# An encoder layer's first modulation vectors computed by column quarters, with the activations loaded from a second DMA queue

## Chip, core and metric

One core of a Trainium2 chip runs the kernel. The metric is the device time of one execution in microseconds, given as the median of three runs. TensorE (PE in the rows, PEld for its weight loads), VectorE (DVE), ScalarE (ACT), GpSimd (POOL) and SyncE (SP) run beside each other and meet at semaphores; transfers are issued from the queues of SP or ACT and carried out by 16 DMA engines. TensorE runs at one of two clocks, 1.2 or 2.4 GHz, and the rows give the granted one as a share of the higher.

## What is computed

One layer of a bidirectional encoder over 1280 tokens (1024 of a sample, 256 of a prompt), width 1024, in float32. Only its beginning matters here:

```python
mod = jax.nn.silu(c) @ ada_w + ada_b
shift1, scale1, gate1, shift2, scale2, gate2 = jnp.split(mod[:, None, :], N_MOD, axis=-1)
h = rms_norm(x, norm_mix_g) * (1 + scale1) + shift1
proj = h @ w_in
```

`ada_w` is 1024 x 6144. The first two vectors, `shift1` and `scale1`, take its first 2048 columns (8 MB), and everything after them needs `h`. Convolution, attention, the output projection and a feed-forward block follow; they are the same in both kernels.

## The kernel before

Tokens are cut into ten tiles of 128 (`xt`, tile t), grouped into chunks c = 0 (tiles 0 to 3), c = 1 (4 to 7) and c = 2 (8 and 9); the width is cut into eight slices of 128, k = 0 to 7. A program order written out by hand decides what stands in each engine's queue; each engine takes its instructions in that order, and a waiting one holds up all behind it.

- **Modulation.** `ada_load(k)` (line 130) loads 128 rows of `ada_w` by 2048 columns, 1 MB, in rows of 8 KB. `ada_products` (line 220) multiplies them by the activated condition `c32`: four matmuls of 512 columns, each into its own 32 partitions of one PSUM bank `aps`. All eight k must be in before `mod_finish` (line 203) can copy the bank out (`rows`), turn it by four transposes (`mps`) and add the bias. `scale_gain` (line 235) then makes the scale vectors `A1`.
- **Normalising x.** `x_load` (line 247) loads a tile of 0.5 MB, `x_norm` (line 252) squares and sums it on ACT and forms the inverse root on POOL, and `x_scale` (line 261) multiplies it on DVE.
- **Turning x.** `h_turn(c, k)` (line 318) transposes slice k of the chunk's tiles on PE; `modulate` (line 264) reads the PSUM bank on ACT with scale and bias (`hf`), makes the high half `Hh` on DVE and the low half `Hl` on DVE for even k and on POOL for odd k.
- **First products.** `passes` (line 327) multiplies one slice by the split weights in three matmuls: wh by Hh, wh by Hl, wl by Hh. Lines 376 to 384 do this for chunks 0 and 1 and the first two column blocks of `w_in` (`w_first`), six matmuls to each (c, k), with three transposed slices ahead of the products. Chunk 2's products (`fmb`) come after.
- **Weights of `w_in`.** They are streamed by `Stream` (line 32): a column block of 128 is loaded as `wr` (0.5 MB, in rows of 512 bytes), copied to `wh` on ACT, and the rest `wl` is formed on POOL.

All these loads are issued from SP's queue, in program order. A transfer takes one of eight completion semaphores, and it is not issued until the transfer that used that semaphore before has landed; these waits stand in the issuing queue like any other.

Of the kernel before, what the change touches and what calls it, by code (L numbers as in the profile page):

```python
# [70 lines left out]
def encoder_kernel(tc, x_prompt, x_sample, c_prompt, c_sample, ada_w, ada_b, norm_mix_g, w_in,  # L71
# [55 lines left out]
    wada = ada_w[0].rearrange("(k p) n -> k p n", p=128)  # L127
    ada_raw = {}

    def ada_load(k):  # L130
        raw = sp.tile([128, 2048], F32, tag="ar", name="ar", bufs=4)
        nc.sync.dma_start(raw, wada[k][:, 0:2048])
        ada_raw[k] = raw

    ada_load(0)
    ident = co.tile([128, 128], F32, name="ident")
# [5 lines left out]
    for k in range(1, 4):  # L142
        ada_load(k)
# [96 lines left out]
    h_cm, hp = pool("h1", side="right")  # L240
    Hh = [hp.tile([128, KD, n], F32R, name=f"Hh{c}") for c, (_, n) in enumerate(CH)]
    Hl = [hp.tile([128, KD, n], F32R, name=f"Hl{c}") for c, (_, n) in enumerate(CH)]
    xp_cm, xp = pool("xp", side="right")
    xts = {}
    xrs = {}

    def x_load(t):
        xt = xp.tile([128, D], F32, tag="xt", name="xt", bufs=8)
        nc.sync.dma_start(xt, x_rows(t))
        xts[t] = xt  # L250

# [30 lines left out]
    aps = bank("t", "aps", 4)  # L282
    for k in range(8):
        raw = ada_raw.pop(k)
        for n in range(4):
            ada_products(aps, k, n, raw[:, n * 512:(n + 1) * 512])
        if k + 4 < 8:
            ada_load(k + 4)
        if k == 3:
            for r0, n, src in vsrc:  # L290
                nc.sync.dma_start(vrow[r0:r0 + n], src)
            for t in range(4):
                x_load(t)
# [3 lines left out]
    A1 = co.tile([128, 8, 2], F32, name="A1")

    x_norm(0)
    turn = mod_finish(0, aps, xp)  # L300
    x_norm(1)
    x_scale(0)
    turn()
    scale_gain(1, "nm", A1)
    x_norm(2)
    x_scale(1)
    x_norm(3)
    x_scale(2)
    x_load(4)
    x_load(5)  # L310
    x_load(6)
    x_load(7)
# [29 lines left out]
    def fmajor(w, Xh, Xl, nk, between=None):  # L342
# [12 lines left out]
    turns = [(c, k) for c in range(3) for k in range(KD)]
    nxt = [0]

    def turns_to(n):
        while nxt[0] < min(n, len(turns)):
# [3 lines left out]
            if c == 0 and k < 4:  # L363
                x_norm(4 + k)
                if k > 0:
                    x_scale(3 + k)
# [1364 lines left out]
```

## Time and profile before

| | |
|---|---|
| median of three runs | 1901.2 us (1901.16 to 1902.71) |
| the profiled execution's own time | 1901.46 us |
| its span | 1899.5 us |
| mean granted clock of TensorE | 0.991 |
| PE busy | 1844.8 us, 97% of the span |
| DVE, ACT, POOL busy | 1073.2, 682.4, 657.2 us |

The span runs from the first to the last instruction of the profiled execution; 1.96 us of its time lie outside. A busy PE may still run at the lower clock, and matmuls are pipelined, so the pace of matmuls is read from the distance between their starts and not from the length of one record.

### The profile page before, as it was taken

To read this page: it belongs to the slowest core of one execution; us is meant where nothing else is said; L and a number is where in the kernel's file an instruction comes from. 1 tells how busy PE (TensorE), PEld (TensorE's weight loads), DVE (VectorE), ACT (ScalarE), POOL (GpSimd) and SP (SyncE) were. 2 spreads that over 40 slices of the span, in tenths; PEclk is the share of its full clock that TensorE was granted. 3 is DMA by queue.
4 is the path that set the end of the run, shared out by engine and by line. 5 is a ranking of instruction groups with operands and counts; after the bars stand their busy time and mean duration, and the time that the engine had idled before them with its cause. 6 is when DMAs were issued, how large, how long until landed. Compare 5 with 4: busy or idle time off the path is not lost.

```text
span 1899.5 us, 24511 instructions
## 1 busy us (share of the span) xinstructions
PE 1844.8 (97%) x9468; PEld 1539.1 (81%) x9468; DVE 1073.2 (57%) x1396; ACT 682.4 (36%) x1132; POOL 657.2 (35%) x491
## 2 busy tenths in 40 slices
PE   5999999999999999998999989999999999999998
PEld 2888777888997888877788878888888888888886
DVE  2799996524346777776455753333334555555557
ACT  3411111221346877774233444444444111111112
POOL 3321121421321343437322013333445444344343
PEclk7999999999999999999999999999999999999999
DMA  8313452227131211116632223222226332233224
GB/s 312 112 43 108 171 185 99 70 99 250 51 98 61 56 41 39 46 56 222 204 122 78 84 100 97 93 95 95 88 91 214 117 100 76 75 100 100 75 93 154
DMA packets 120933, 207.54 MB, mean 109 GB/s; under 512 B 10946, under 2 KB 78355, under 8 KB 119794
## 3 DMA queue, kind: packets, MB, share of 16 engines
q1 hardware_dynamic: 103106, 167.32, 27.7%
q10 hardware_dynamic: 17712, 38.67, 5.2%
q8 instruction: 74, 1.21, 0.3%
q14 instruction: 41, 0.34, 0.1%
HBM read 151.83 MB, written 54.12 MB: 108 GB/s over the span
## 4 chain that ended last, share of the span: by engine, by line
PE 85%; DVE 4%; DMA 4%; ACT 3%; POOL 2%; issue 1%; SPq 1%; ACTq 0%; POOLq 0%; DVEq 0%
PE dn_ps L1583 23%; PE up_ps L1444 14%; PE fma L328 5%; PE fma L330 5%; PE fma L329 5%; PE wo_ps L1198 5%; PE tp L866 3%; PE up_ps L330 2%; PE up_ps L329 2%; PE up_ps L328 2%; PE fmb L328 1%; PE fmb L330 1%; PE fmb L329 1%; PE pq L668 1%; PE pq L666 1%
## 5 line engine op out<-in xcount | busy, mean ns | idle before, releaser
L160 POOL TENSOR_TENSOR wl<-wr,wh 128x1024 fp32r<-128x1024 f32 (+1 forms) x100 | 235.4, 2354 | 728.7 <-ACT wh L156 705.8
L1598 DVE TENSOR_TENSOR acc<-acc,dn_ps 128x512 f32<-128x512 f32 x260 | 178.7, 687 | 174.9 <-PE dn_ps L1583 174.9
L1583 PE MATMUL dn_ps<-wh,gl 128*128 128x512 f32 x640 | 249.1, 389 | 0.9 <-POOL gl L160 0.9
L1583 PE MATMUL dn_ps<-wh,gh 128*128 128x512 f32 x640 | 249.0, 389 | 0.0
L1583 PE MATMUL dn_ps<-wl,gh 128*128 128x512 f32 x640 | 249.0, 389 | 0.0
L156 ACT ACTIVATE wh<-wr 128x1024 fp32r<-128x1024 f32 (+1 forms) x104 | 102.9, 991 | 381.5 <-PE dn_ps L1583 291.0
L412 DVE SCALAR_TENSOR_TENSOR z<-u,dwt,z 128x1310 f32<-128x1310 f32 x120 | 220.8, 1840 | 4.3
L328 PE MATMUL fma<-Hh,wh 128*128 128x512 f32 x384 | 154.9, 403 | 0.3 <-DVE Hh L158 0.3
L329 PE MATMUL fma<-Hl,wh 128*128 128x512 f32 x384 | 150.6, 392 | 2.0 <-DVE Hl L160 2.0
L330 PE MATMUL fma<-Hh,wl 128*128 128x512 f32 x384 | 150.5, 392 | 0.0
L1583 PEld LDWEIGHTS dn_ps<-wh,gl 128*128 128x128 f32 x640 | 120.1, 188 | 26.5 <-POOL gl L160 1.4
L1583 PEld LDWEIGHTS dn_ps<-wl,gh 128*128 128x128 f32 x640 | 120.1, 188 | 24.9
L1583 PEld LDWEIGHTS dn_ps<-wh,gh 128*128 128x128 f32 x640 | 120.1, 188 | 24.8
L160 DVE TENSOR_TENSOR Pl<-tp,Ph 128x512 fp32r<-128x512 f32 x144 | 92.8, 649 | 20.2 <-ACT Ph L156 19.1
L160 POOL TENSOR_TENSOR gl<-gr,gh 128x1280 fp32r<-128x1280 f32 x32 | 94.7, 2960 | 11.9 <-DMA up_d<-r 9.7
L328 PE MATMUL up_ps<-Mh,wh 128*128 128x256 f32 (+1 forms) x320 | 97.4, 304 | 0.8 <-ACT hf L266 0.8
L329 PE MATMUL up_ps<-Ml,wh 128*128 128x256 f32 (+1 forms) x320 | 97.4, 304 | 0.0
L330 PE MATMUL up_ps<-Mh,wl 128*128 128x256 f32 (+1 forms) x320 | 97.4, 304 | 0.0
L156 ACT ACTIVATE Ph<-tp 128x512 fp32r<-128x512 f32 x144 | 82.4, 574 | 36.0 <-PE tp L866 33.2
L1444 PE MATMUL up_ps<-Mh,wh 128*128 128x512 f32 x224 | 88.2, 394 | 5.4 <-ACT p L1457 5.4
L328 PEld LDWEIGHTS fma<-Hh,wh 128*128 128x128 f32 x384 | 72.6, 189 | 23.3 <-issue 5.0
L1444 PE MATMUL up_ps<-Ml,wh 128*128 128x512 f32 x224 | 88.0, 393 | 0.0
(327 smaller groups left out, 4306.6 us busy)
## 6 DMA issues: line engine op xcount, KB each, us to landing
gr<-up_d SPq DMA_DIRECT2D x32, 640.0 KB
adr<-in_ada_w_dram SPq DMA_DIRECT2D x32, 512.0 KB
wr<-in_w_mlp_up_dram SPq DMA_DIRECT2D x32, 512.0 KB
up_d<-r ACTq DMA_DIRECT2D x64, 256.0 KB
wr<-in_w_mlp_down_dram SPq DMA_DIRECT2D x32, 512.0 KB
wr<-in_w_in_dram SPq DMA_DIRECT2D x24, 512.0 KB
ar<-in_ada_w_dram SPq DMA_DIRECT2D x8, 1024.0 KB
sig_a<-sgg ACTq DMA_DIRECT2D x8, 640.0 KB
```

What stands on the lines that cost most here:

```text
L156: nc.scalar.activation(h, raw, AF.Copy)
L160: e.tensor_tensor(l, raw, h.bitcast(F32), op=ALU.subtract)
L328: nc.tensor.matmul(o, lhsT=wh, rhs=xh, start=first, stop=False)
L329: nc.tensor.matmul(o, lhsT=wh, rhs=xl, start=False, stop=False)
L330: nc.tensor.matmul(o, lhsT=wl, rhs=xh, start=False, stop=last)
L412: nc.vector.scalar_tensor_tensor(out=z[j], in0=u[j][:, t:t + ZW], scalar=dwt[:, j, t:t + 1], in1=z[j], op0=ALU.mult, op1=ALU.add)
L666: nc.tensor.matmul(pq, lhsT=xh, rhs=wh, start=(k == 0), stop=False)
L866: nc.tensor.transpose(tp[:, i * 128:(i + 1) * 128], st_[n]["P"][i][:, k * 128:(k + 1) * 128], ident)
L1198: nc.tensor.matmul(pp[hf], lhsT=a, rhs=wo[k][b][:, hf * 512:hf * 512 + 512], start=(k == 0 and s == 0), stop=(k == KD - 1 and s == 2))
L1444: nc.tensor.matmul(out, lhsT=l_, rhs=r_[:, k, :], start=(a and s == 0), stop=(b and s == 2), skip_group_check=more)
L1583: nc.tensor.matmul(pds[hf], lhsT=l_, rhs=r_, start=(i == 0 and s == 0), stop=(i == nf - 1 and s == 2), skip_group_check=bool(early))
L1598: nc.vector.tensor_add(acc[t][:, cs], acc[t][:, cs], pds[hf])
```

## The change

The first 2048 columns of `ada_w` are loaded by quarters of each vector's columns: quarter q is two tiles of [128, 8, 256], all 1024 rows by 256 columns of `shift1` and of `scale1`, 1 MB each, in rows of 1 KB. `ada_quarter(q)` multiplies all eight k of a quarter (32 matmuls of 128 columns), copies the bank, transposes it once, and gives the slices k = 2q and 2q + 1 of `mods[0]`, `mods[1]` and `A1`. The transposed slices and the first products of these two k follow before the next quarter. x is loaded from ACT's queue, with ten buffers in place of eight; the first four tiles are loaded at the start, the others on the way. The third and fourth weight block are loaded after the last quarter of `ada_w`.

```diff
+    wcol = ada_w[0].rearrange("(k p) n -> p k n", p=128)
-    def ada_load(k):
-        raw = sp.tile([128, 2048], F32, tag="ar", name="ar", bufs=4)
-        nc.sync.dma_start(raw, wada[k][:, 0:2048])
-        ada_raw[k] = raw
+    def ada_load(q):
+        if q < 4:
+            ada_raw[q] = []
+            for m in range(2):
+                raw = sp.tile([128, KD, 256], F32, tag="ar", name="ar", bufs=4)
+                nc.sync.dma_start(raw, wcol[:, :, m * D + q * 256:m * D + q * 256 + 256])
+                ada_raw[q].append(raw)
     ada_load(0)
...
+        xt = xp.tile([128, D], F32, tag="xt", name="xt", bufs=10)
+        nc.scalar.dma_start(xt, x_rows(t))
...
+    for t in range(4):
+        x_load(t)
...
-    aps = bank("t", "aps", 4)
-    for k in range(8):
-        raw = ada_raw.pop(k)
-        for n in range(4):
-            ada_products(aps, k, n, raw[:, n * 512:(n + 1) * 512])
...
+    for r0, n, src in vsrc:
+        nc.sync.dma_start(vrow[r0:r0 + n], src)
+    WS.prefetch()
+    WS.raw_bufs = 0
+    ada_load(1)
+    for t in range(4, 8):
+        x_load(t)
...
+    def x_ready(t):
+        x_norm(t)
+        x_scale(t)
+
+    def ada_quarter(q):
+        raw = ada_raw.pop(q)
+        aps = bank("t", "aps", 4, (128, 128))
+        for k in range(KD):
+            for n in range(4):
+                nc.tensor.matmul(aps[n * 32:n * 32 + 32, :], lhsT=c32[:, k, :],
+                                 rhs=raw[n // 2][:, k, (n % 2) * 128:(n % 2) * 128 + 128],
+                                 start=(k == 0), stop=(k == KD - 1))
+        if q == 0:
             v_turn()
+        ada_load(q + 2)
+        rows = xp.tile([128, 128], F32, tag="rows", name="rows", bufs=2)
+        nc.scalar.activation(rows, aps, AF.Copy)
+        mps = bank("t", "mps", 4, (128, 128))
+        nc.tensor.transpose(mps, rows, ident)
...
+    for t in range(4):
+        x_ready(t)
+    w_first = [WS.get(R_in[0]), WS.get(R_in[1], 0)]
     dwrow = sp.tile([CK, CW], F32, name="dwrow")
-    nc.sync.dma_start(dwrow, conv_dw[0])
-    x_scale(3)
-    w_first = [WS.get(R_in[0]), WS.get(R_in[1], 0)]
+    nc.scalar.dma_start(dwrow, conv_dw[0])
+    x_load(8)
+    x_load(9)
...
+    for q in range(4):
+        k0, k1 = 2 * q, 2 * q + 1
+        ada_quarter(q)
+        h_turn(0, k0)
+        h_turn(0, k1)
+        if q == 0:
+            for t in range(4, 8):
+                x_ready(t)
+        if q == 1:
+            x_ready(8)
+            x_ready(9)
+        h_turn(1, k0)
+        first_two(0, k0)
+        h_turn(1, k1)
+        first_two(0, k1)
+        if q > 1:
+            h_turn(2, 4 * q - 8)
+            h_turn(2, 4 * q - 7)
+        first_two(1, k0)
+        if q > 1:
+            h_turn(2, 4 * q - 6)
+        first_two(1, k1)
+        if q > 1:
+            h_turn(2, 4 * q - 5)
+    WS.raw_bufs = 2
+    WS.prefetch()
```

`first_two(c, k)` is the six matmuls of lines 380 to 383. On ACT, from the first squares on, the kernel before has this order (`junk,ss<-xt` is the square of an x tile, `rows` the copy of the modulation bank, `wh` a weight's high half, `hf` the modulated slice):

```order
L256 ACTIVATE junk,ss<-xt 128x1024
L206 ACTIVATE rows<-aps 128x512
L256 ACTIVATE junk,ss<-xt 128x1024 x3
L156 ACTIVATE wh<-wr 128x1024 x2
L266 ACTIVATE hf<-xt_ps,mod_118,A_200 128x512
L256 ACTIVATE junk,ss<-xt 128x1024
L266 ACTIVATE hf<-xt_ps,mod_118,A_200 128x512
L256 ACTIVATE junk,ss<-xt 128x1024
L266 ACTIVATE hf<-xt_ps,mod_118,A_200 128x512
```

The changed kernel has this in the same place of ACT's queue, from the loads of tiles 4 to 7 on:

```order
L150 DMA xt<-in_x_sample_dram 128x1024 x4
L261 ACTIVATE junk,ss<-xt 128x1024 x4
L173 ACTIVATE wh<-wr 128x1024 x2
L330 DMA dwrow<-in_conv_dw_dram 31x512
L150 DMA xt<-in_x_prompt_dram 128x1024 x2
L312 ACTIVATE rows<-aps 128x128
L271 ACTIVATE hf<-xt_ps,mod_134,A_164 128x512 x2
L261 ACTIVATE junk,ss<-xt 128x1024 x4
L271 ACTIVATE hf<-xt_ps,mod_134,A_164 128x512 x2
L312 ACTIVATE rows<-aps 128x128
```

The squares of tiles 0 to 3, both weight halves and three DMA issues now stand ahead of the first `rows`, and the squares of tiles 4 to 7 stand in one piece between the second and the third `hf`.

The next piece is SP's queue in the changed kernel from the first quarter to the second; in brackets are the semaphores waited for. `ar` is a half of a quarter of `ada_w`, `vrow` the small vectors, `wr` the weights; DMAHW3 and DMAHW6 are first used by the two halves of the first quarter, DMAHW0, 4, 5 and 7 by x tiles 0 to 3:

```order
L137 DMA ar_91<-in_ada_w_dram 128x8x256
L137 DMA ar_93<-in_ada_w_dram 128x8x256
L288 DMA vrow_124<-in_norm_mix_g_dram 8x128 [waits DMAHW0_49]
...
L288 DMA vrow_124<-in_conv_dw_b_dram 4x128 [waits DMAHW3_49]
L288 DMA vrow_124<-in_conv_ln_g_dram 4x128 [waits DMAHW4_49]
L288 DMA vrow_124<-in_conv_ln_b_dram 4x128 [waits DMAHW5_49]
...
L288 DMA vrow_124<-in_ada_b_dram 48x128 [waits DMAHW1_49]
L184 DMA wr_148<-in_w_in_dram 128x8x128 [waits DMAHW3_49]
L184 DMA wr_150<-in_w_in_dram 128x8x128 [waits DMAHW5_49]
L137 DMA ar_152<-in_ada_w_dram 128x8x256 [waits DMAHW6_49]
L137 DMA ar_154<-in_ada_w_dram 128x8x256 [waits DMAHW7_49]
```

And ACT's queue in the changed kernel at the loads of tiles 4 to 7 (`xt_156` to `xt_162`), ahead of the first square:

```order
L150 DMA xt_156<-in_x_sample_dram 128x1024
L150 DMA xt_158<-in_x_sample_dram 128x1024 [waits DMAHW6_49]
L150 DMA xt_160<-in_x_sample_dram 128x1024 [waits DMAHW2_49]
L150 DMA xt_162<-in_x_sample_dram 128x1024 [waits DMAHW4_49]
L261 ACTIVATE junk_165,ss_166<-xt_107 128x1024 [waits DMAHW0_49]
```

The load of tile 5 (`xt_158`) waits for the second half of the first quarter to land, that of tile 7 (`xt_162`) for a `vrow` that SP issues after the first half has landed; the first square stands behind them.

On PE, from the modulation products on, the kernel before has this order (`xt_ps` are transposes of x; Hh_127 and Hl_130 are chunk 0's halves):

```order
L222 MATMUL aps<-ar,c_100 32x512 x32
...
L211 MATMUL mps<-ident,rows 128x128 x4
L323 MATMUL xt_ps<-ident,xt 128x128 x12
L328 MATMUL fma<-Hh_127,wh 128x512
L329 MATMUL fma<-Hl_130,wh 128x512
L330 MATMUL fma<-Hh_127,wl 128x512
...
L323 MATMUL xt_ps<-ident,xt 128x128 x8
```

The changed kernel has this on PE where the first quarter's products end and the second quarter begins (Hh_98 and Hl_101 are chunk 0's halves, Hh_99 chunk 1's):

```order
L346 MATMUL fma<-Hh_99,wl 128x512
L305 MATMUL aps<-ar,c_122 32x128 x32
L314 MATMUL mps<-ident,rows 128x128
L339 MATMUL xt_ps<-ident,xt 128x128 x12
L344 MATMUL fma<-Hh_98,wh 128x512
L345 MATMUL fma<-Hl_101,wh 128x512
L346 MATMUL fma<-Hh_98,wl 128x512
...
L339 MATMUL xt_ps<-ident,xt 128x128 x4
```

Between two quarters' products PE now has 32 modulation matmuls, one transpose of `rows`, and twelve transposes of x, and the first product after them needs an `hf` made from that `rows`.

## Rows read from the trace of the kernel before

**Rows 1.** From the page, the head of the profile page: span and instructions, then TensorE's (PE) busy time, share of the span and instructions.

```profile
span 1899.5 us, 24511 instructions
...
PE 1844.8 (97%) x9468; PEld 1539.1 (81%) x9468; DVE 1073.2 (57%) x1396; ACT 682.4 (36%) x1132; POOL 657.2 (35%) x491
```

**Rows 2.** From the trace, busy time by stretch (start:end, its length; then busy us and count on PE, PEld, DVE, ACT and POOL; the granted TensorE clock as a share of full; the share of the DMA engines; GB/s).

```profile
6.46:25.70 19.24, 14.53 (x65) 1.71 (x65) 0.03 (x1) 0.00 (x0) 0.00 (x0) 0.82 0.90 373
25.70:37.94 12.24, 4.73 (x16) 3.05 (x16) 4.49 (x10) 8.67 (x14) 6.16 (x10) 0.62 1.05 385
37.94:45.72 7.78, 5.81 (x17) 4.55 (x18) 7.19 (x8) 5.20 (x10) 7.23 (x9) 0.50 0.64 197
45.72:73.53 27.81, 27.07 (x149) 22.14 (x148) 20.18 (x34) 16.16 (x27) 13.95 (x16) 1.00 0.17 58
...
76.70:200.00 123.30, 123.14 (x657) 102.79 (x657) 118.84 (x74) 17.62 (x21) 29.79 (x22) 1.00 0.30 95
```

**Rows 3.** From the trace, the chain that ended last, from 23 to 46 us: start, length, and the work (queue, engine or transfer) that it went through.

```profile
15.47 8.00 DMA ar<-in_ada_w_dram
...
26.23 9.04 DMA wr<-in_w_in_dram
...
35.29 1.06 ACT wh L156
...
37.92 2.74 DVE Hl L160
...
40.70 0.80 PE fma L329
41.50 0.43 PE fma L330
...
43.21 1.71 PE xt_ps L323 x8
```

**Rows 4.** From the trace, the DMA engines from 0 to 40 us in slices of one microsecond: the rate of each slice in GB/s.

```profile
GB/s 0 4 135 229 418 451 410 426 434 434 410 426 434 434 410 426 442 434 401 442 434 426 349 4 49 225 393 389 352 381 372 329 346 378 422 406 426 422 323 284
```

**Rows 5.** From the trace, PE from 73 to 78 us: the last product of the two large chunks and the first of the small one.

```profile
73.52 0.39 PE L330 MATMUL fma<-Hh,wl 128*128 128x512 f32 x1
73.75 0.28 PE L328 MATMUL fmb<-Hh,wh 128*128 128x256 f32 x1
```

**Rows 6.** From the trace, transfers issued from SyncE's queue (SPq), in order of time: start, length of the issuing, destination and source, count.

```profile
23.85 1.84 SPq L249 DMA_DIRECT2D xt<-in_x_sample_dram  x4
25.74 2.54 SPq L167 DMA_DIRECT2D wr<-in_w_in_dram  x2
28.32 5.42 SPq L249 DMA_DIRECT2D xt<-in_x_sample_dram  x4
```

**Rows 7.** From the trace, all engines from 28 to 36 us, in order of time: start, length, engine, line, operation, operands, count, and in brackets what the engine had waited for.

```profile
28.50 0.58 ACT L206 ACTIVATE rows<-aps 128x512 f32<-128x512 f32 x1
...
30.28 0.25 DVE L217 TENSOR_TENSOR mod<-mps,vt 128x16 f32<-128x16 f32 x2
...
30.57 0.17 DVE L237 SCALAR_TENSOR_TENSOR A<-mod,vt 128x16 f32<-128x16 f32 x1
...
31.07 1.06 ACT L256 ACTIVATE junk<-xt 128x1024 f32<-128x1024 f32 x1 [0.96 <-DMA xt<-in_x_sample_dram]
...
32.36 1.06 ACT L256 ACTIVATE junk<-xt 128x1024 f32<-128x1024 f32 x1
...
33.32 0.19 ACT L256 ACTIVATION_READ_ACCUMULATOR junk<-xt 128x1 f32 x1
...
34.04 0.55 POOL L181 TENSOR_TENSOR rs<-rs,neghalf 128x1 f32<-128x1 f32 x1
34.62 0.75 DVE L262 TENSOR_SCALAR xt<-xt,rs 128x1024 f32<-128x1024 f32 x1 [0.71 <-POOL rs L181]
```

**Rows 8.** From the trace, the matmuls that transpose x, over the first 76 us: count, then shortest, median and longest in ns, and the first and last start.

```profile
L323 PE MATMUL xt_ps<-ident,xt x80: 270/273/477, 30.4 to 70.9; 128*128 128x128 f32 x80
```

**Rows 9.** From the trace, all engines from 43 to 51 us: the modulation step (hf) and its split into a high and a low half.

```profile
43.12 0.41 DVE L158 CAST Hh<-hf 128x512 fp32r<-128x512 f32 x1
...
43.57 0.69 DVE L160 TENSOR_TENSOR Hl<-hf,Hh 128x512 fp32r<-128x512 f32 x1
...
44.16 0.78 ACT L266 ACTIVATE hf<-xt_ps,mod,A 128x512 f32<-128x512 f32 x1 [1.60 <-PE xt_ps L323]
...
45.48 1.29 POOL L160 TENSOR_TENSOR Hl<-hf,Hh 128x512 fp32r<-128x512 f32 x1
```

**Rows 10.** From the trace, the chain from 45.7 to 50 us: product matmuls and the transposes of x at full clock.

```profile
47.18 0.23 PE fma L328
47.41 0.23 PE fma L329
...
48.57 0.87 PE xt_ps L323 x8
```

**Rows 11.** From the trace, PE from 18.5 to 21 us: the modulation products of one eighth of the rows (four matmuls of 512 columns, two records each), with the clock at half.

```profile
18.60 1.94 PE L222 MATMUL aps<-ar,c 128*32 128x512 f32 x8 [1.37 <-DMA ar<-in_ada_w_dram]
```

**Rows 12.** From the trace, PE from 162.9 to 164.5 us: the same four matmuls of a later modulation row, at full clock.

```profile
163.15 1.06 PE L222 MATMUL adps<-adr,c 128*32 128x512 f32 x8
164.15 0.50 PE L328 MATMUL fma<-Hh,wh 128*128 128x512 f32 x1
```

More of the change, by code (lines that the diff above doesn't have):

```diff
@@ L141, in encoder_kernel @@
     nc.gpsimd.memset(c32, 0.0)
-    for k in range(1, 4):
-        ada_load(k)
     vrow = sp.tile([81, 128], F32, name="vrow")
@@ L237, in scale_gain @@
         nc.vector.scalar_tensor_tensor(out=out, in0=mods[m], scalar=1.0, in1=g, op0=ALU.add, op1=ALU.mult)
[L240 to L250, printed above, removed]
     def x_norm(t):
@@ L297, in encoder_kernel @@
[L297 to L312, printed above, removed]
+    for r0, n, src in vsrc:
[5 more added lines that the diff above has]
+        x_load(t)
+    A1 = co.tile([128, 8, 2], F32, name="A1")
@@ new lines, in x_ready @@
+    def x_ready(t):
[10 more added lines that the diff above has]
+        if q == 0:
+            v_turn()
+        ada_load(q + 2)
[3 more added lines that the diff above has]
+        nc.tensor.transpose(mps, rows, ident)
+        ks = slice(2 * q, 2 * q + 2)
+        pv = mps.rearrange("p (m b x) -> p m b x", m=2, b=2)
+        for m in range(2):
+            b0 = VO["ab"] + m * 8 + 2 * q
+            nc.vector.tensor_tensor(mods[m][:, ks, :], pv[:, m, :, 0:2],
+                                    vt[:, b0:b0 + 2].unsqueeze(2).to_broadcast([128, 2, 2]), op=ALU.add)
+        g0 = VO["nm"] + 2 * q
+        nc.vector.scalar_tensor_tensor(out=A1[:, ks, :], in0=mods[1][:, ks, :], scalar=1.0,
+                                       in1=vt[:, g0:g0 + 2].unsqueeze(2).to_broadcast([128, 2, 2]),
+                                       op0=ALU.add, op1=ALU.mult)
@@ L352, in fmajor, with first_two @@
         return pa, pb
[L355 to L359, printed above, removed]
-            c, k = turns[nxt[0]]
-            nxt[0] += 1
-            h_turn(c, k)
[L363 to L366, printed above, removed]
-            if c == 0 and k == 4:
-                x_scale(7)
-            if c == 0 and k == 7:
-                x_load(8)
-                x_load(9)
-            if c == 1 and k in (0, 1):
-                x_norm(8 + k)
-                x_scale(8 + k)
     pas = [bank("a", "fma", 2, (128, 1024)) for _ in range(2)]
     pb0 = bank("t", "fmb", 4, (128, 256))
-    turns_to(3)
-    for c in range(2):
-        for k in range(KD):
-            for i in range(2):
-                wh, wl = w_first[i]
-                passes(pas[i][:, c * 512:(c + 1) * 512], wh[:, k, :], wl[:, k, :], Hh[c][:, k, :], Hl[c][:, k, :],
-                       k == 0, k == KD - 1)
-            turns_to(3 + (3 * (c * KD + k + 1) + 1) // 2)
-    turns_to(24)
+    def first_two(c, k):
+        for i in range(2):
+            wh, wl = w_first[i]
+            passes(pas[i][:, c * 512:(c + 1) * 512], wh[:, k, :], wl[:, k, :], Hh[c][:, k, :], Hl[c][:, k, :],
+                   k == 0, k == KD - 1)
+    for q in range(4):
[24 more added lines that the diff above has]
+    WS.prefetch()
     for k in range(KD):
```

17 lines of the change are left out of this document (8 added, 9 removed).

## The prediction

> **What bounds the kernel now.** I read the page's head first: PE is busy for 97% of a span of 1899.5 us [rows 1], so only work on PE's path counts. Then the stretches at the start, where the change lies. Until 37.94 us PE does the modulation products and waits [rows 2]; the first product of `passes` stands at 37.94. From there to 45.72 the clock is at half; from 45.72 to 73.53 PE is busy for 27.07 of 27.81 us at full clock, and after 76.70 for 123.14 of 123.30 [rows 2]. So once the products run, PE is the bound, and nothing later has slack in which a shift of this beginning could vanish: what the first stage gains or loses the kernel gains or loses. The chain says what holds the first product: the load of the eight 1 MB pieces up to 23.47 us, x and the first weights behind it up to 35.27, the weight split, the first `hf`, and then a `Hl` of 2.74 us [rows 3]. The transfers come at 426 to 434 GB/s with rows of 8 KB, at 352 to 393 with x's rows of 4 KB (slices 26 to 29), and at 329 to 346 with the weights' 512 bytes (slices 31 and 32) [rows 4]. The stage's end, by which I measure, is the first `fmb`, at 73.75 us [rows 5].
>
> **When the first product comes after the change.** The PE order puts the transposes of tiles 4 to 7 ahead of it, and ACT's queue puts nearly everything ahead of those, so I add up ACT's queue.
>
> The first quarter (2.10 MB) and tiles 0 to 4 (2.62 MB) are in flight together, 4.72 MB. Rows of 1 KB are not in the trace; bounds are 430 GB/s and 335 [rows 4], and I take 385, between x's rate and the weights'. From about 2.9 us on, where the rate rises, that is 12.3 us: the quarter's second half lands at **15.2 us** (13.9 to 17.0). ACT cannot issue tile 5 before that, and its squares stand behind these issues.
>
> The Trainium skill, "DMA: Bandwidth & Descriptors", Specifications, states that transfers run at line rate from 512 bytes a row on. By that the landing would be at 13.9 and the sum below 1.3 us less; the slices with 512-byte rows, at 329 to 346, do not agree with it. The same page (Issuing engines are not separate DMA queues) says that a second queue saves only issue time, since all transfers share 16 engines; the trace agrees in so far as one queue already fills them, with a share of 1.05 [rows 2].
>
> From 15.2 on, on ACT: three issues at 0.46 (SP takes 1.84 for four [rows 6]), 16.6. Four squares at a pitch of 1.29 (31.07 to 32.36 [rows 7]), 21.8. The two `wh` of 1.06 [rows 3]; their loads are issued only when small vectors queued behind the first quarter have landed, so at about 16.6, and share the engines with tiles 5 to 7: 2.62 MB at 370 GB/s from 17 on are in at 24.1, so the second `wh` ends at 25.2 (23.9 if nothing is waited for). Three issues, 26.6. `rows`, 128 of 512 columns of a 0.58 us copy, about 0.3; one transpose at half clock 0.48 [rows 8]; modulation and scale vectors 0.46 (30.28 to 30.74 [rows 7]): 27.8. Two `hf` of 0.78 [rows 9], 29.4. The four squares of tiles 4 to 7, 5.2: 34.6. Then the last tile's root and scaling, from the read-out's end at 33.51 to 35.37 in the trace [rows 7], 1.9, and its transpose at half clock, 0.2. The first product starts at **36.7 us** (34.1 to 38.5), 1.2 us earlier than before. The loads have become much earlier, but most of that is lost, because ACT's list of about 21.5 us starts only once the first quarter is in.
>
> **What PE then has to do.**
> - Products and transposes that were there before: 96 matmuls at a pitch of 0.231 and 68 transposes at 0.109 [rows 10], 22.2 + 7.4 = **29.6 us**. Before the change the same work took 73.75 - 37.94 = 35.8 us, 6.2 of them lost to the half clock and the long `Hl`.
> - Half clock at the beginning. The chain has a product at 0.43 there [rows 3]. In the kernel before, products ran without a break from 40.70, and the clock rose at 45.72 [rows 2, 3]: 5.0 us at half pace, **2.5 us** lost. I take the same.
> - The modulation products of quarters 1 to 3, which used to run under the loads. At full clock four matmuls of 512 columns take 1.06 us, at half 1.94 [rows 11, 12]; a quarter is eight such groups at a fourth of the columns, 2.1 or 3.9. Shorter matmuls may hide their weight loads less well; I take 2.5, nearer to the full-clock row. Three times, **7.5 us** (6.4 to 11.6). The first quarter's products lie under ACT's list and cost nothing.
> - A gap behind each of these. The next product needs `rows` (0.3), a transpose (0.27 [rows 8]), modulation and scale (0.46), `hf` (0.78), `Hh` (0.41) and some six handovers of 0.03 (34.59 to 34.62 [rows 7]): 2.4 us after the last modulation product. Twelve transposes, 1.3, fill part of it. Its second matmul then waits for `Hl` on DVE, 0.69 against 0.23 [rows 9, 10]. 1.1 + 0.5 = 1.6 us, three times **5.0 us** with the handovers. If other work filled it, nothing; at half clock about 2.5 each.
> - Quarter 1 alone has the squares of tiles 8 and 9 on ACT (2.6) ahead of chunk 1's `hf`, and their scaling on DVE, behind POOL's `Hl` of 1.29 [rows 9], ahead of chunk 1's `Hh`. Chunk 1's products come 1.5 us late, and its two low halves cost some 0.9 more: **2.4 us** (0 to 4).
>
> The loads bound none of this: the second quarter is in by about 31 us and the third by about 39, and PE asks for them at about 45 and 58; the fourth is issued when the second's products are done, at about 47, and is in by 55, against some 71. The weight blocks 2 and 3 follow it and are split only after the stage. `v_turn` lies under ACT's list as well.
>
> **Sum.** 29.6 + 2.5 + 7.5 + 5.0 + 2.4 = 47.0 us. The first `fmb` comes at 36.7 + 47.0 = 83.7 us in place of 73.75: 9.9 us later. With 1901.46 for the profiled execution that is 1911.4; the median of the runs lies 0.26 below it: **1911 us**, slower by 0.5%. My measure of no change is 0.2%, 3.8 us.
>
> **Rivals.**
> - *The clock falls in the gaps.* After PE had stood still the trace has the clock at 0.62 of full from 25.70 to 37.94 and at half to 45.72 [rows 2]. Against it: from 45.72 on short waits of PE left the clock at full [rows 2]. If each of the three gaps brings a stretch like the first, 2.5 us each, the time is 1918.5. Chance 0.14.
> - *The gaps close and the start is early.* The landing at 13.9, weights that are not waited for (first product at 34.1), modulation products at 2.1 each, and half of the 7.4 us of gaps and waits gone: 34.1 + 29.6 + 2.5 + 6.4 + 3.7 = 76.3, 2.6 us later than before, 1904, no change that can be measured. For it: DVE and POOL have room; against it: each step of the gap needs the one before. Chance 0.16.
> - *Faster: ACT's list starts while the first quarter is still coming.* Tiles 0 to 3 land from about 6 us on, and were ACT not held by the issue of tiles 5 to 7, its squares would be done 5 to 7 us sooner. With 47.0 us of work behind it, the first product has to come before 26.7 us for the kernel to gain, and before 22.9 for 0.2%. From the list's 21.5 us that means a start at 5.2 and 1.4 us, by when 4.72 MB cannot be in at any rate of [rows 4]; so the work behind would have to be shorter as well, close to the 29.6 + 2.5 + 6.4 = 38.5 us that remain without any gap. With a first product 6 us earlier, 30.7, and 38.5 behind it the stage ends at 69.2, 4.5 us earlier: 1896.7. Chance 0.07.
> - *The second queue does not do what it says.* Only tiles 0 to 4 run beside the first quarter; tiles 5 to 7 wait for it through the semaphores. That is in the sum already.
>
> **How the numbers follow.** The forecast (slower, 1906 to 1916) has 0.63, the fallen clock 0.14, both slower: 0.77. Within 0.2% has 0.16, faster 0.07. The predicted time is the forecast's. The range leaves out the faster case, the lower half of the unchanged one and a part of the fallen clock: 1903.5 to 1918.5.
>
> **What the profile would show.** The square of tile 0 at about 16.6 us and not at 6; the first `fma` product at 34 to 38.5; 32 modulation matmuls in 2 to 4 us ahead of each later quarter; behind each a PE gap ended by `Hh` or `Hl`; the first `fmb` near 84 us; all after it as before, moved by one amount. I am wrong if the first product stands below 30 us, if the clock is at half after some 42 us, if PE waits for an `ar` load in quarters 1 to 3, or if the later stages are not moved by what the first lost.

## The result, and the profile after

| | before | after |
|---|---|---|
| median | 1901.23 us (4 runs) | 1915.49 us (4 runs, 1913.59 to 1916.98) |
| ratio, 95% interval | | 1.0071 [1.0056, 1.0085] |
| span of the profiled execution | 1899.5 us | 1911.5 us |
| first product | 37.94 us | 38.66 us |
| first `fmb` | 73.75 us | 85.71 us |

The change makes the kernel slower by 0.7%. A second series of five gave 1913.7 us (below); the median of the nine is **1914.1**, and the experiments are compared with that.

The head of the page after, span and PE's busy time:

```profile
span 1911.5 us, 24904 instructions
...
PE 1843.7 (96%) x9660; PEld 1546.2 (81%) x9660; DVE 1067.5 (56%) x1405; ACT 682.9 (36%) x1135; POOL 658.2 (34%) x491
```

PE is busy for 1.1 us less than before ([rows 1] has 1844.8 us) and the span is 12.0 us longer: the time went into standing still. Where, the first 90 us show.

ACT after, in order of time (start, length, operation, operands, count; in brackets the idle time and what ended it):

```profile
14.96 1.30 ACTq L150 DMA_DIRECT2D xt<-in_x_sample_dram  x3
16.30 1.06 ACT L261 ACTIVATE junk<-xt 128x1024 f32<-128x1024 f32 x1 [10.29 <-DMA vrow<-in_kv_norm_g_dram]
...
22.84 1.06 ACT L173 ACTIVATE wh<-wr 128x1024 fp32r<-128x1024 f32 x1 [1.84 <-DMA wr<-in_w_in_dram]
24.41 1.06 ACT L173 ACTIVATE wh<-wr 128x1024 fp32r<-128x1024 f32 x1 [0.51 <-DMA wr<-in_w_in_dram]
...
25.82 0.28 ACT L312 ACTIVATE rows<-aps 128x128 f32<-128x128 f32 x1 [0.36 <-issue]
...
33.61 1.06 ACT L261 ACTIVATE junk<-xt 128x1024 f32<-128x1024 f32 x1
```

The first square stands at 16.30 us, behind three transfers that ACT issues from 14.96 to 16.26 (ACTq); the second `wh` ends at 25.47, `rows` stands at 25.82, the last square of tiles 4 to 7 begins at 33.61. What follows it, all engines from 34.5 us on:

```profile
34.57 0.18 ACT L261 ACTIVATION_READ_ACCUMULATOR junk<-xt 128x1 f32 x1
34.80 0.75 DVE L267 TENSOR_SCALAR xt<-xt,rs 128x1024 f32<-128x1024 f32 x1 [0.72 <-POOL rs L198]
34.85 0.75 POOL L197 TENSOR_SCALAR rs<-ss 128x1 f32<-128x1 f32 x1
...
35.68 0.55 POOL L198 TENSOR_TENSOR rs<-rs,neghalf 128x1 f32<-128x1 f32 x1
36.26 0.75 DVE L267 TENSOR_SCALAR xt<-xt,rs 128x1024 f32<-128x1024 f32 x1 [0.71 <-POOL rs L198]
...
37.73 0.75 DVE L267 TENSOR_SCALAR xt<-xt,rs 128x1024 f32<-128x1024 f32 x1 [0.71 <-DMA ar<-in_ada_w_dram]
...
38.54 0.47 PE L339 MATMUL xt_ps<-ident,xt 128*128 128x128 f32 x1 [0.99 <-DVE xt L267]
...
38.66 0.77 PE L344 MATMUL fma<-Hh,wh 128*128 128x512 f32 x1
```

The square's sum is read out until 34.75. Each scaling on DVE (`xt`) waits for its root on POOL (`rs`); the last row names a load, but the root before it ended at 37.70, 0.03 us earlier. POOL's 128x1 TENSOR_SCALAR takes 0.75 us where a scaling runs beside it, and 0.19 where none does (32.47, below). So the tiles come every 1.47 us, the last one 3.9 us after the last square, and the first product with it, at 38.66. Before, it stood at 37.94 [rows 3].

PE after (aps: modulation products; 64 records are one quarter's 32 matmuls):

```profile
14.98 3.63 PE L305 MATMUL aps<-ar,c 128*32 128x128 f32 x60 [1.97 <-DMA ar<-in_ada_w_dram]
...
47.31 1.95 PE L305 MATMUL aps<-ar,c 128*32 128x128 f32 x64
49.69 0.33 PE L314 MATMUL mps<-ident,rows 128*128 128x128 f32 x1 [0.42 <-ACT rows L312]
...
51.89 0.51 PE L344 MATMUL fma<-Hh,wh 128*128 128x512 f32 x1 [0.56 <-DVE Hh L175]
52.62 0.50 PE L345 MATMUL fma<-Hl,wh 128*128 128x512 f32 x1 [0.22 <-DVE Hl L177]
...
57.83 0.50 PE L344 MATMUL fma<-Hh,wh 128*128 128x512 f32 x1 [1.96 <-DVE Hh L175]
...
61.62 1.96 PE L305 MATMUL aps<-ar,c 128*32 128x128 f32 x64
...
73.75 1.95 PE L305 MATMUL aps<-ar,c 128*32 128x128 f32 x64
...
85.71 0.37 PE L344 MATMUL fmb<-Hh,wh 128*128 128x256 f32 x1
```

From 38.66 on a quarter takes 8.7, 14.3, 12.1 and 12.0 us. Each later quarter begins with 1.96 us of modulation products, and its first `fma` comes 2.6 us after they end, first behind `Hh`, then behind `Hl`. In quarter 1 chunk 1 waits another 1.96 us for `Hh` at 57.83: on DVE the scalings of tiles 8 and 9 stand ahead of that `Hh`, the second one here:

```profile
56.69 0.75 DVE L267 TENSOR_SCALAR xt<-xt,rs 128x1024 f32<-128x1024 f32 x1 [0.72 <-POOL rs L198]
```

The first `fmb` at 85.71 is 11.96 us later than in [rows 5], and the span grew by 12.0. Busy time by stretch (columns as in [rows 2]):

```profile
50.00:60.00 10.00, 7.03 (x36) 4.89 (x33) 4.72 (x11) 4.97 (x8) 4.42 (x6) 1.00 0.97 315
...
90.00:200.00 110.00, 110.00 (x583) 92.16 (x582) 106.20 (x64) 14.01 (x17) 25.96 (x14) 1.00 0.29 91
```

In the fifties PE stands still for 3 of 10 us; from 90 to 200 us it is busy without a gap, as before [rows 2]. That the span grew by as much as the first `fmb` came later shows that nothing of the loss was given back.

### The profile page after: what moved, and what is told of

Read it like the earlier page. It is cut to its first block, busy times and chain, and to the rows that moved or that the text cites. A ratio compares the mean times of both kernels' runs of the same rounds, so it can differ in the third digit from the quotient of the medians.

```text
span 1911.5 us, 24904 instructions
## 1 busy us (share of the span) xinstructions
PE 1843.7 (96%) x9660; PEld 1546.2 (81%) x9660; DVE 1067.5 (56%) x1405; ACT 682.9 (36%) x1135; POOL 658.2 (34%) x491
## 3 DMA queue, kind: packets, MB, share of 16 engines
q8 instruction: 76, 1.25, 0.3%
## 4 chain that ended last, share of the span: by engine, by line
PE 54%; DVE 4%; ACT 3%; DMA 2%; POOL 2%; issue 1%; ACTq 0%; SPq 0%; POOLq 0%; DVEq 0%
PE dn_ps L1604 23%; PE up_ps L1465 14%; PE wo_ps L1219 4%; PE tp L887 2%; PE up_ps L346 2%; PE up_ps L345 1%; PE up_ps L344 1%; PE ops L902 1%; PE ops L901 1%; PE S L872 1%; PE S L871 1%; PE S L873 1%; DMA ga<-sig_a 1%; ACT P L879 1%; POOL m L1172 0%
## 5 line engine op out<-in xcount | busy, mean ns | idle before, releaser
L1604 PEld LDWEIGHTS dn_ps<-wl,gh 128*128 128x128 f32 x640 | 120.1, 188 | 25.2
```

What stands on the lines that cost most here:

```text
L1604: nc.tensor.matmul(pds[hf], lhsT=l_, rhs=r_, start=(i == 0 and s == 0), stop=(i == nf - 1 and s == 2), skip_group_check=bool(early))
```

## The experiments

"After" is the changed kernel. Times are medians; the kernel before ran beside them at 1901.1 to 1901.4 us.

**The changed kernel again.** No edit.

> The changed kernel once more, unaltered, as the base for the runs beside it and to see where its median of 1915.5 lies above its first profiled execution of 1913.6. Theory (its beginning always costs 12 us, and the rest comes from where the clock is at half in a single execution): first product at 38.5 to 38.8, first fmb at 85.2 to 85.8, 1912 to 1916. Rival (the beginning itself varies): the first fmb differs by more than 1 us.

1913.7 us (1911.3 to 1914.69), ratio 1.0062 [1.0049, 1.0075]. First product again at 38.66, first `fmb` at 85.90. The beginning is the same to 0.2 us, but by two differences that cancel: quarter 0 was 1.1 us shorter (full pace from 41.8 on in place of 44.0), and quarter 1 1.1 us longer. Its stretches in quarter 1:

```profile
57.00:60.00 3.00, 2.77 (x9) 1.81 (x9) 0.72 (x2) 0.00 (x0) 1.29 (x1) 0.77 0.50 153
60.00:62.00 2.00, 2.00 (x12) 1.13 (x15) 0.00 (x0) 0.00 (x0) 0.00 (x0) 0.50 0.03 8
```

Behind the waits of quarter 1 the granted clock falls to half (0.50), and products stand 0.43 us apart until 61.57. In the first profile it stays at full in the same place.

**x from SP's queue.**

```diff
-        nc.scalar.dma_start(xt, x_rows(t))
+        nc.sync.dma_start(xt, x_rows(t))
```

> The changed kernel with one line undone: x is loaded from SP's queue again, everything else as changed. Theory (ACT's list decides when the first product comes, and its own queue of transfers holds it): without transfers in its queue ACT squares the first tile when that tile lands, at 8 to 13 us in place of 16.3; the list is then held by the weights instead (second wh at about 23 to 24.5), so the first product comes at 36 to 38 in place of 38.66, and the time is 1911 to 1914 against 1915.5, a gain of at most 3 us. The 47 us behind the first product stay. Rival (the second queue is what makes the loads early, and without it they come late): first product at 41 or later, 1918 or more. Rival (the second queue is the cause of the loss): the time falls back to about 1901 to 1905.

1909.95 us (1909.54 to 1912.29), 4.1 less than after, more than the 3 us expected; first product at 37.47, as expected, first `fmb` at 83.61, the span 3.6 us shorter. ACT of this run:

```profile
10.62 1.06 ACT L261 ACTIVATE junk<-xt 128x1024 f32<-128x1024 f32 x1 [6.47 <-DMA xt<-in_x_sample_dram]
...
30.04 1.06 ACT L261 ACTIVATE junk<-xt 128x1024 f32<-128x1024 f32 x1 [4.42 <-DMA xt<-in_x_sample_dram]
```

Without transfers in its queue ACT starts at 10.62 in place of 16.30. But the squares of tiles 4 to 7 begin at 30.04 as before (30.07), now held 4.42 us by the load of x, which stands behind the second quarter in SP's queue. So ACT's hold was real, but removing it alone mostly moved the wait. With the squares at the same place, the first product is 1.2 us earlier because POOL is free when the first root of these tiles is due (shown in the section on the prediction). The rival that the second queue brings the loads forward is refuted: the first quarter, no longer beside x, has its remaining products begin at 9.40 us in place of 14.98. The one that it is the whole loss is refuted too: 8.8 us remain.

**x from ACT's queue in the kernel before.**

```diff
-        nc.sync.dma_start(xt, x_rows(t))
+        nc.scalar.dma_start(xt, x_rows(t))
```

> The kernel before with one line changed: x is loaded from ACT's queue, nothing else. Theory: the loss comes from the order of the products on PE and not from the queue; the eight 1 MB pieces and the first tiles share the 16 engines, all together are in at about the same time as before (35 us), and the first product comes at 36 to 39 against 37.94: 1899 to 1904. Rival (the second queue is the cause of the loss): 1908 or more, the first product 7 us or more later.

1903.59 us (11 runs), ratio 1.0013 [1.0004, 1.0022], as the theory has it; the first product at 39.51 is later than its 36 to 39, and the first `fmb` at 76.75 is 3.0 us later than before. The second queue costs the old kernel 2.4 us. With the run before, its share of the 13 us is some 2 to 4.

**One eighth of the later modulation products.**

```diff
+        nk = KD if q == 0 else 1
-        for k in range(KD):
+        for k in range(nk):
```

> The changed kernel with the modulation products of quarters 1 to 3 cut to the first of their eight k (4 matmuls in place of 32; their vectors are then not the reference's). Theory (these products lie on PE's path at 1.96 us a quarter): each quarter loses seven eighths, 1.7 us, three times 5.1 us: the first fmb at about 80.6 in place of 85.7, and 1910 to 1911. Rival (PE would wait for something else in that time, ACT's or DVE's list, and the products are covered): less than 1.5 us in all, 1914 or more.

1910.59 us (1910.07 to 1912.19), 3.5 less, as expected; first `fmb` at 81.89, 3.8 us earlier, where 5.1 were expected. Four matmuls took 0.43 us, so 3 x (1.96 - 0.43) = 4.6 us of PE's work went; some 1 us came back: the clock fell to half behind quarter 1's waits here as well (0.57 of full from 57 to 60). The products do lie on PE's path.

**No vectors of the later quarters.**

```diff
-        ... A1[:, k, g:g + 1], mods[0][:, k, g:g + 1], ...
+        ... A1[:, k % 2, g:g + 1], mods[0][:, k % 2, g:g + 1], ...
```

> The changed kernel, in which every slice is modulated by the first quarter's vectors (k mod 2), so that no slice waits for a later quarter's rows, transpose and scale vectors; the products of all quarters are still made (the result differs). Theory (behind each later quarter's products PE waits 2.6 us for the chain rows, transpose, vectors, hf, Hh, Hl): rows still stands ahead of hf on ACT but nothing waits for the vectors on DVE; of 2.6 us some 1.4 to 1.6 go each time, 4 to 5 us in all: first fmb at about 81, 1910 to 1911.5. Rival (the gap is hf, Hh and Hl behind the six or twelve transposes, whatever the vectors): less than 1.5 us in all, 1914 or more.

1912.64 us, 1.5 less; the first `fmb` at 85.20, 0.5 earlier, most of it from the earlier full pace in quarter 0 (from 43.4). The gap stayed: 2.57 us for 2.63. But ACT and DVE of this run show that the edit did not take the wait away:

```profile
49.00 0.28 ACT L312 ACTIVATE rows<-aps 128x128 f32<-128x128 f32 x1 [5.74 <-PE aps L305]
50.18 1.45 ACT L271 ACTIVATE hf<-xt_ps,mod,A 128x512 f32<-128x512 f32 x2 [0.91 <-DVE A L322]
```

```profile
49.96 0.16 DVE L322 SCALAR_TENSOR_TENSOR A<-mod,vt 128x4 f32<-128x4 f32 x1
```

`hf` still starts behind the scale vectors `A` (50.12), although it reads two other columns of that tile: in this program the wait goes by the whole tile. The run is inconclusive on its question.

**Chunk 0's products ahead of tiles 4 to 7.**

```diff
         if q == 0:
+            first_two(0, k0)
+            first_two(0, k1)
             for t in range(4, 8):
                 x_ready(t)
```

> The changed kernel with the first quarter's products of chunk 0 ahead of the squares, scalings and transposes of tiles 4 to 7; the rest as changed. Theory (tiles 4 to 7 hold the first product through ACT, POOL and DVE): the first product comes at 30.5 to 31 in place of 38.66, and its 12 matmuls at half clock are done before the last tile is scaled at about 37.7; chunk 1 then starts at about 40: first fmb at 81 to 83.5 in place of 85.7, 1909 to 1912. Rival (what ends the quarter is tile 7 and not the products): first product early, first fmb earlier by less than 1 us.

1911.93 us, 2.2 less. PE of this run:

```profile
30.32 0.79 PE L344 MATMUL fma<-Hh,wh 128*128 128x512 f32 x1 [1.69 <-DVE Hh L175]
...
38.87 1.33 PE L339 MATMUL xt_ps<-ident,xt 128*128 128x128 f32 x5 [1.14 <-DVE xt L267]
40.68 0.80 PE L344 MATMUL fma<-Hh,wh 128*128 128x512 f32 x1 [0.48 <-DVE Hh L175]
...
46.03 1.96 PE L305 MATMUL aps<-ar,c 128*32 128x128 f32 x64
```

The first product comes 8.3 us earlier, the first `fmb` (84.46) only 1.25, below the 2.2 to 4.7 of the theory and just above the rival's 1. The quarter ends when tile 7 has come and passed through `hf`, `Hh` and `Hl`, with chunk 1's twelve products behind it, at half pace almost to their end (40.68 to 46.03; the granted clock is 0.56 from 42 to 46). So the first product's time was not the right measure of quarter 0; the rival had the mechanism.

**Looking one quarter ahead.** `ada_quarter` is cut in two: `ada_mm` (products, copy) and `ada_vec` (transpose, vectors).

```diff
     for q in range(4):
         first_two(0, k0)
         h_turn(1, k1)
...
+        if q < 3:
+            ada_mm(q + 1)
         first_two(0, k1)
...
         first_two(1, k0)
...
+        if q < 3:
+            ada_vec(q + 1)
+            h_turn(0, k0 + 2)
+            h_turn(0, k1 + 2)
         first_two(1, k1)
```

> The changed kernel with the modulation products of quarter q + 1, its bank copy, its transpose and its vectors put between the products of quarter q, and the transposes of chunk 0 of quarter q + 1 ahead of the last product of quarter q; the same instructions in all. Theory (PE waits behind each later quarter's products for the copy, hf, Hh and Hl, 1.2 us, and for tiles 8 and 9 in quarter 1, 2.0 us): the three waits go and most of quarter 1's: first product as before at 38.6, first fmb at 80 to 82, 1908 to 1911. Rival (the waits only move, since the copy and hf stand behind the same PE work): first fmb at 84.5 or later, 1913 or more.

1905.89 us (10 runs), 8.2 less than after, ratio to before 1.0023 [1.0014, 1.0033]. PE of this run:

```profile
42.36 2.61 PE L307 MATMUL aps<-ar,c 128*32 128x128 f32 x64
...
52.51 1.96 PE L307 MATMUL aps<-ar,c 128*32 128x128 f32 x64
...
79.11 0.37 PE L350 MATMUL fmb<-Hh,wh 128*128 128x256 f32 x1
```

The same instructions, the first product at 38.67 as after, and the first `fmb` 6.6 us earlier, more than expected. Behind the modulation products nothing waits now; waits of 0.2 us at 60.9, 71.5 and 72.3 are left. The gaps and quarter 1's wait together are the largest single piece of the loss. (The profiled execution, 1908.88 us, is the slowest of the ten, and its span is only 4.7 us shorter than after's: 1.9 us of the 6.6 are lost again later, by a cause that stays open.)

**Both orders, and the beginning put right.** x from SP, the small vectors issued first from ACT, x tiles 4 to 7 ahead of the second quarter, the first weights split behind the first quarter's copy in place of ahead of it, chunk 0 first, one quarter ahead. The excerpt shows only the loads.

```diff
+    for r0, n, src in vsrc:
+        nc.scalar.dma_start(vrow[r0:r0 + n], src)
     ada_load(0)
...
     for t in range(4, 8):
         x_load(t)
+    ada_load(1)
```

> Both of these orders, x from SP's queue, the small vectors issued first from ACT's queue, x tiles 4 to 7 ahead of the second quarter and the weights ahead of these. The modulation products of quarters 1 to 3 remain on PE (5.9 us). Theory (the quarters lose by what stands ahead of the first product and by the waits behind each quarter, not by their loads): the first product comes at 20 to 24, PE then has 38 us of work and some 4 to 8 us of waits (tiles 4 to 7, half clock): first fmb at 62 to 70, 1890 to 1898, faster than the kernel before. Rival (the loads bound it: 14.2 MB at 380 GB/s are in at 40, and waits for quarters 2 and 3 appear): PE waits for an ar load, first fmb at 72 or later, 1899 or more.

1896.95 us (9 runs), ratio to before **0.9976 [0.9967, 0.9986]**: with quarters and with all their products on PE the kernel is faster than before. First product at 24.14, first `fmb` at 70.14, both just past the late end of what was expected. DVE and POOL show one cause:

```profile
17.70 2.83 DVE L269 TENSOR_SCALAR xt<-xt,rs 128x1024 f32<-128x1024 f32 x1 [0.71 <-POOL rs L200]
...
21.05 1.70 DVE L332 SCALAR_TENSOR_TENSOR A<-mod,vt 128x4 f32<-128x4 f32 x1
```

```profile
17.63 5.10 POOL L179 TENSOR_TENSOR wl<-wr,wh 128x1024 fp32r<-128x1024 f32 x2
```

Beside POOL's split of the weights (`wl`, 17.63 to 22.73) a scaling takes 2.83 us in place of 0.75, and the scale vectors 1.70 in place of the 0.16 that they take later.

**Roots by pairs of tiles.**

```diff
-            for t in range(4, 8):
-                x_ready(t)
+            x_pair(4)
+            x_pair(6)
+    def x_pair(t):
+        ss = co.tile([128, 2], F32, tag="ss2", name="ss2", bufs=5)
+        rs = co.tile([128, 2], F32, tag="rs2", name="rs2", bufs=5)
...
```

> The changed kernel with the inverse roots of tiles 4 to 7 formed on POOL for two tiles at once (two square sums side by side, one root, then both scalings on DVE); the rest as changed. Theory (each root on POOL waits for the scaling of the tile before on DVE, 1.47 us a tile, and the last scaling ends 3.7 us after the last square): root 0.75 to 1.3 and two scalings of 0.75 after the last square at 34.75, so the last transpose at 37.0 to 37.6 and the first product there, 1 to 1.6 us earlier than 38.66; first fmb 84.2 to 84.9 against 85.7, 1912 to 1913.5. Rival (the scaling waits for something else, such as POOL's Hl of 1.27): the first product at 38.3 or later.

1922.98 us, 9 us **more** than after, which neither theory foresaw. In the stage itself the edit did most of what was expected: from the last square's read-out to the first product it takes 2.7 us (3.9 in after). But the last square was read out 0.7 us later, at 35.4, so the first product at 38.11 is only 0.55 us earlier, between the theory's 37.6 and the rival's 38.3; the first `fmb` is 1.3 us earlier than after. PE:

```profile
37.98 0.47 PE L349 MATMUL xt_ps<-ident,xt 128*128 128x128 f32 x1 [0.19 <-DVE xt L308]
38.11 0.78 PE L354 MATMUL fma<-Hh,wh 128*128 128x512 f32 x1
...
84.40 0.37 PE L354 MATMUL fmb<-Hh,wh 128*128 128x256 f32 x1
```

So the loss lies elsewhere; the last two runs bear on that.

**The kernel before with early loads.** No quarters; small vectors first, x tiles 0 to 3 and the weights behind the first four pieces, all preparation while the rest is loaded.

```diff
     for k in range(1, 4):
         ada_load(k)
+    for t in range(4):
+        x_load(t)
...
+    WS.prefetch()
+    for t in range(4):
+        x_norm(t)
+        x_scale(t)
+    w_first = [WS.get(R_in[0]), WS.get(R_in[1], 0)]
     aps = bank("t", "aps", 4)
```

> The kernel before, by rows and without quarters, with the small vectors issued first from ACT's queue, x tiles 0 to 3 and the two weight blocks loaded behind the first four pieces of the modulation matrix, tiles 4 to 7 behind the last, and the squares, scalings and weight splits done while the matrix is loaded. Theory (what makes the kernel before late is that x and the weights come behind the 8 MB, and the quarters are not needed to mend that): the last piece lands at about 30.5, its products end at 32 to 32.5, rows, transposes, vectors, hf and Hh 3.5 us: first product at 35 to 36.5, without the low half's wait of 2 us behind the weights' split; first fmb at 69 to 71.5, 1895 to 1899. Rival (the later tiles take the place of the wait): first fmb at 73 or later, 1900.5 or more.

1898.04 us (11 runs), ratio 0.9988 [0.9979, 0.9997]. PE:

```profile
31.68 1.61 PE L238 MATMUL aps<-ar,c 128*32 128x512 f32 x8 [0.50 <-DMA ar<-in_ada_w_dram]
...
36.57 0.51 PE L322 MATMUL fma<-Hh,wh 128*128 128x512 f32 x1 [0.58 <-DVE Hh L174]
...
70.34 0.28 PE L322 MATMUL fmb<-Hh,wh 128*128 128x256 f32 x1
```

The last eighth's products begin at 31.68, the first product comes at 36.57, just past the expected 36.5, and is not followed by the wait of [rows 3]; the first `fmb` stands 3.4 us earlier than before. Early loads without quarters give 3.1 us, where the run with quarters and both orders gave 4.4.

**Pairs, the first weights split on DVE, and tiles 8 and 9 made ready in the first quarter.** The excerpt is against the run with both orders.

```diff
-    for t in range(4, 8):
-        x_ready(t)
+    x_pair(4)
+    x_pair(6)
...
+    x_pair(8)
...
-            x_ready(8)
-            x_ready(9)
...
-    R_in = [w_add(win[:, :, c:c + 128], [128, KD, 128]) for c in COLS]
+    R_in = [w_add(..., "v" if i < 2 else "g") for i, c in enumerate(COLS)]
```

> The kernel with both orders and early vectors once more, with three edits: roots by pairs of tiles, the low halves of the first two weight blocks formed on DVE in place of POOL, and tiles 8 and 9 made ready in the first quarter in place of the second. In the run before, a scaling on DVE took 2.83 us and the scale vectors 1.70 beside POOL's weight split, and the transposes of tiles 4 to 7 came at 29.7, 31.2 and 32.7. Theory (POOL's long work stretches DVE's, and the pair of engines steps tile by tile): first product at 21 to 23 in place of 24.14, tiles 4 to 7 turned by 28 to 29, the clock up before 30: first fmb at 63 to 67 in place of 70.14, 1890 to 1894. Rival (DVE's own list, longer by 2.7 us, takes its place): first product at 24 or later, first fmb at 69 or later, 1896 or more.

1905.55 us (11 runs): 8.6 more than the run that it builds on, while its first `fmb` stands at 66.31, 3.8 us earlier, as expected. Both runs with `x_pair` gain in the stage and lose 10 to 12 us behind it. What they share outside it is the place of the tiles in SBUF: ten small buffers ahead of the weights.

**The tiles back in place.**

```diff
-        ss = co.tile([128, 2], F32, tag="ss2", name="ss2", bufs=5)
-        rs = co.tile([128, 2], F32, tag="rs2", name="rs2", bufs=5)
+        ss = co.tile([128, 2], F32, tag="ss2", name="ss2", bufs=4)
+        rs = co.tile([128, 2], F32, tag="rs2", name="rs2", bufs=4)
```

> The last kernel again with four buffers in place of five for the two small tiles of the pairs, and nothing else. These tiles stand ahead of the weights in SBUF: with five buffers each the weights' tiles begin 320 bytes further than in the kernel before (64 bytes past a multiple of 128), with four 256 bytes further (at a multiple of 128). The two runs with five buffers had an earlier first fmb and yet lost some 10 us later: 438 to 439 matmuls in each 100 us of the last stage in place of 443. Theory (the place of the weights in SBUF slows every product): 443 again, the first fmb at 66.3 as with five buffers, and 1892 to 1895 in place of 1905.6. Rival (the root of two columns or the order of the first stage costs it): 438 to 439 again, 1904 to 1907.

**1892.38 us** (1892.19 to 1893.81), ratio to before **0.9955 [0.9941, 0.9968]**: 13.2 us less than with five buffers, and the best version of all. The two kernels differ in nothing else. One stretch of the last stage, first with five buffers, then with four:

```profile
1600.00:1700.00 100.00, 100.00 (x439) 82.04 (x438) 50.24 (x73) 17.34 (x16) 42.22 (x16) 1.00 0.26 88
```

```profile
1600.00:1700.00 100.00, 100.00 (x443) 82.79 (x442) 50.44 (x74) 13.07 (x13) 39.25 (x15) 1.00 0.29 95
```

PE is busy throughout in both, at full clock, and starts 439 or 443 matmuls. The kernel before and the profiles of all ten other runs without five such buffers have 443 there too; the changed kernel with pairs has 438. It was not run with four buffers, so for it the cause is read from this number and not shown. Over some 1800 us 0.9% are 16 us if all products bore it; behind the first `fmb` the two spans (1904.0 and 1890.5 us) differ by 12.6 us. So the number of buffers is shown to cost the time; that it does so by the place of what is allocated behind them is the reading that is left, since PE waits for nothing in either stretch; which of those tiles bears it is not shown. PE's first stage in the last run:

```profile
21.89 0.80 PE L359 MATMUL fma<-Hh,wh 128*128 128x512 f32 x1 [1.97 <-DVE Hh L177]
...
29.51 1.96 PE L321 MATMUL aps<-ar,c 128*32 128x128 f32 x64
...
65.42 0.36 PE L359 MATMUL fmb<-Hh,wh 128*128 128x256 f32 x1
```

The first product at 21.89, quarters of about 10 us, the first `fmb` at 65.42: 8.3 us earlier than before, and the median 9.0. Pairs and the split on DVE were not tried without the quarters, so how much of the 9.0 the quarters themselves give stays open.

## Why the prediction was right, point by point

**When the first product comes** was forecast as 36.7 (34.1 to 38.5) and measured as 38.66. The list on ACT held at its ends: the rest of the first quarter at 15.2 against 14.98, first square 16.6 against 16.30, second `wh` 25.2 against 25.47, last square 34.6 against 34.75. (By the Trainium skill's line rate, "DMA: Bandwidth & Descriptors", Specifications, the quarter would by estimate have been in at 13.9, 1.1 us earlier than the trace has it.) Between the second `wh` and the last square it held by luck. ACT issued its last transfers beside the second `wh`, and the squares came every 1.18 us in place of 1.29; but the scale vectors, which the forecast had at 0.17 us, took 1.71 beside POOL's weight split:

```profile
26.93 1.71 DVE L322 SCALAR_TENSOR_TENSOR A<-mod,vt 128x4 f32<-128x4 f32 x1
```

The mis-sized term is the last tile's root, scaling and transpose. I took 1.9 + 0.2 us from the row of a single tile [rows 7], and it was 3.9. Two things make the difference. Four tiles in a row step through POOL and DVE in turns, at 1.47 us a tile where the squares come every 1.18. And POOL still has chunk 0's odd `Hl` ahead of the first root, a term that the forecast had in quarter 1 and not here. POOL after, then in the run with x from SP:

```profile
31.12 1.27 POOL L177 TENSOR_TENSOR Hl<-hf,Hh 128x512 fp32r<-128x512 f32 x1 [2.49 <-DVE Hh L175]
32.47 0.19 POOL L197 TENSOR_SCALAR rs<-ss 128x1 f32<-128x1 f32 x1
```

```profile
31.27 0.19 POOL L197 TENSOR_SCALAR rs<-ss 128x1 f32<-128x1 f32 x1 [3.46 <-ACT junk L261]
```

The square of tile 4 is read out at 31.2 in both. Where that `Hl` was done earlier, the first product came 2.6 us after the last square: 0.5 us of the excess is the stepping, and the other 1.3 is `Hl`. The pairs brought it to 2.7; their first root needs two squares and so comes after `Hl` anyway, so that run does not separate the two. The Trainium skill, "SBUF — State Buffer", SBUF: two separate sides, calls the port pair that DVE (in some kinds of instruction) and GpSimd share an exclusive lock, held for a whole instruction; the 0.19 us instruction that lasts 0.75 beside a scaling, and the scaling of 2.83 beside POOL's split, agree with that.

**What PE then has to do** was forecast as 47.0 and measured as 47.05. That the two agree so closely is luck, since the parts are off by up to 1.6 us and cancel:

| | forecast | measured |
|---|---|---|
| half clock | 2.5 | 2.7 (half pace from 38.66 to 44.0, by the distance of the starts) |
| modulation products | 7.5 | 5.9 (3 x 1.96) |
| gaps behind them | 5.0 | 5.5 (2.63 less twelve transposes at 0.109, plus 0.5 for `Hl`; three times) |
| quarter 1's tiles 8 and 9 | 2.4 | 3.1 (14.31, less 12.05 for quarters 2 and 3 without their eight transposes) |

With the 29.6 us of work that was there before, this is 46.8. For the first row the clock column of this profile is no help: it reads 1.00 from 36 to 50 us, while the starts are 0.43 us apart until 43.9; in the second profile, at the same pace, it reads 0.55 from 38 to 42. That the products lie on PE's path is shown by the run with an eighth of them; that the gaps and the waits of quarter 1 are empty time, by the look ahead, which took 6.6 us out with the same instructions. The chain inside a gap (copy, vectors, `hf`, `Hh`, `Hl`) is read from the rows; the run meant to cut it did not.

**The sum** gave 1911 us, 4.5 below the median of the first series, which lies in the stated range; the profiled execution took 1913.6: 1.96 us of that is the later first product. The other eight executions lie between 2.3 us lower and 3.4 us higher, with granted clocks of 0.986 to 0.996. In the one of them that was profiled the clock fell behind quarter 1 and was lower from 850 to 950 us (0.90 and 0.93, against 1.00 and 0.97); that these make the whole spread is not shown. One sign that the forecast named against itself did appear: half pace after some 42 us, until 44.0, since the products began 2 us late, and in the second profile again from 58.5 to 61.6.

**The rivals.** *The clock falls in the gaps*: not in the first profile, but in two of the later ones, in quarter 1 alone, for about 1 us each. The mechanism exists and its price was set too high. *The gaps close*: not in this order; with one quarter of look-ahead they do. *Faster*: ACT was not free before 16.3 us, and freeing it alone was not enough; it took the other orders as well. In the last run the first product came at 21.89 and 43.5 us of work followed, and the kernel gained, as that rival's arithmetic asked (a first product before 22.9 with 47 us behind it, or less work behind). *The second queue does not do what it says*: the forecast had ACT's hold in its sum but gave it no price; the two runs price the queue at 2.4 and 4.1 us.

## What to carry to other kernels

Work that used to run under the loads is not free when a change moves it among products on a busy engine: count it, and put the step that unlocks the next block one block ahead, since the same instructions in that order gave 8 of the 13 us back here. Measure such a stage by its last wait and not by its first product: 8.3 us at the front were worth 1.25 at the end. After an edit that adds a small tile, compare matmuls per 100 us of a stage that it does not touch.

## What was not expected of the hardware

- **The place of the tiles behind ten small buffers.** With five buffers each the weights, and the tiles allocated behind them, begin 64 bytes past a multiple of 128, with four at a multiple of 128 (as in the kernel before): 439 against 443 matmuls in 100 us at full clock, 1905.55 against 1892.38 us. Only these two offsets were run; which of the tiles bears the cost, and what in the chip makes it, stay open.
- **DVE and POOL hold each other up, for times like those of whole instructions**: beside POOL's split of 2.3 to 2.8 us 0.75 us became 2.83 on DVE and 0.16 became 1.70, and beside a scaling of 0.75 us 0.19 became 0.75 on POOL.
- **The clock fell to half behind quarter 1's waits** in one profile of the changed kernel and not in the other, at the same place of the same program.
